# Attention's probabilities turned by DMA transposes of 16-bit halves instead of TensorE, two steps later, in a two-layer hybrid decoder trunk

## The chip, the cores and the metric

The kernel runs on one core of one Trainium2 chip. A core has TensorE (PE; its weight loads are listed apart as PEld), VectorE (DVE), ScalarE (ACT), GpSimd (POOL) and SyncE (SP, which here only issues DMAs); the on-chip memory SBUF with 128 partitions; and PSUM, where TensorE leaves its results. The metric is the device time of one execution in microseconds.

## The reference

Two layers over 512 tokens of width 1024, all float32. A layer is half a SwiGLU feed-forward (inner width 2816), then attention and a short convolution side by side behind one common projection, then another half feed-forward:

```python
x = x + 0.5 * swiglu(rms_norm(x, ffn1_norm[l]), ffn1_wg[l], ffn1_wu[l], ffn1_wd[l])
h = rms_norm(x, mix_norm[l])
z = h @ w_in[l]                      # q 8x64, k 2x64, v 2x64, conv B, C, h 512 each
attn_out = sliding_window_attention(q, k, v, attn_sink[l])
conv_out = short_conv(z[..., V_END:CB_END], z[..., CB_END:CC_END], z[..., CC_END:CH_END], conv_w[l])
x = x + jnp.concatenate([attn_out, conv_out], axis=-1) @ w_out[l]
x = x + 0.5 * swiglu(rms_norm(x, ffn2_norm[l]), ffn2_wg[l], ffn2_wu[l], ffn2_wd[l])
```

The attention has 8 query heads on 2 key heads and a window of 128 tokens, so a block of 128 queries sees its own block of keys and the one before it. A bias falls with distance, and each head has a learned sink in the denominator:

```python
scores = jnp.where(mask_b, scores + bias, -jnp.inf)
m = jnp.maximum(jnp.max(scores, axis=-1, keepdims=True), sink_l)
p = jnp.where(mask_b, jnp.exp(scores - m), 0.0)
denom = jnp.sum(p, axis=-1, keepdims=True) + jnp.exp(sink_l - m)
out = jnp.einsum("bnkgqs,bnskd->bnqkgd", p / denom, v_band)
```

## The kernel before

Activations lie with features on the partitions and tokens along the row. TensorE takes its operands as fp32r; each is split into a rounded part `hi` and a rest `lo`, and a product is made of three matmuls (hi·hi, lo·hi, hi·lo). `split` does this: ScalarE casts to `hi` (L223), VectorE subtracts to get `lo` (L224). For weights these tiles are called `wh` and `wl`, three buffers each.

Weights are loaded in 512 KB units into tiles `raw` of a pool of eight buffers (`stock`, tag "raw"). `need_raw` issues the loads on SP (L206) four units ahead of their split, and some on GpSimd's queue, which add to a tile that is there already (L218, L290). `take_split` asks for the split of a unit two groups before TensorE needs it.

The stage that the change touches is `mix`, once in each layer. `group` (L319, L320, L322) makes one 128-column block of the projection: 24 matmuls of 128x512 into one PSUM tile `acc`. The blocks come in the order k, v, four of q, and then twelve of the convolution (C, C, h, h, B, B for two pairs of blocks). After each block comes one "step" of attention, `attend(step)`; the steps from 6 on are made by `go_on`, which also asks for the next split, issued after the last instruction that `attend` returned.

Attention's work is cut into eight units (`Unit`, `todo`): key head g is 0 or 1 and query block n is 0 to 3, n running fastest. A unit has four heads. Its stages, each with a list of steps (`SCORES_AT`, `TURN_AT`, `VALUES_AT`), are:

- `scores`: 16 short matmuls into two PSUM tiles `sc`, VectorE adds the bias and takes the maximum (L1528), small VectorE instructions make `nm` and `es` (L1539, L1541), ScalarE takes the exponentials (L1545, and the sink's in L1548), VectorE adds up and inverts `sums` (L1549, L1550) and scales `p` (L1553). `p` is a tile of the "raw" pool, with queries on the partitions. It covers two blocks of keys, or one where n is 0.
- `turn`: keys have to lie on the partitions for the next product. For each block of keys, four TensorE transposes (L1561) bring `p` into PSUM `pt`, ScalarE casts it to `ph` (L1564), VectorE subtracts to `pl` (L1565).
- `values`: two matmuls for each block of keys (L1576, L1577) into `o`, ScalarE copies half of it to `ol` (L1579), VectorE adds both halves into `mixed` (L1582).

The convolution's elementwise work lies between: VectorE multiplies an `acc` into `cc` and `ch` (L1630, L1637), ScalarE and VectorE make the taps (L1639, L1641, L1642), GpSimd adds and scales (L1645, L1646), VectorE multiplies once more (L1650). Except in marked stretches, the order of each engine's instructions is laid down when the kernel is built, from priorities and assumed durations; at run time each engine takes its own in that order and waits on semaphores.

DMA transposes of 16-bit halves stand in the feed-forward already: `lay_apart` (L138, ScalarE) writes the two 16-bit halves of each word into two rows, a transpose is issued on SP for 1024 half words a partition (L1117), and ScalarE's copy (`join`, L1133) puts the halves together again.

Of the kernel before, what the change touches and what calls it, by code (L numbers as in the profile page):

```python
# [8 lines left out]
F32 = mybir.dt.float32  # L9
F32R = mybir.dt.float32r  # L10
BF16 = mybir.dt.bfloat16
U16 = mybir.dt.uint16
# [4 lines left out]
P = 128  # L17
# [36 lines left out]

SENT_AT = {3: (0, 0), 4: (1, 1)}
SCORES_AT = (5, 6, 7, 8, 9, 10, 12, 13)
TURN_AT = (6, 7, 8, 10, 11, 12, 14, 15)
VALUES_AT = (7, 8, 9, 11, 12, 13, 15, 16)
WARM = 3
XT_TAGS = ("sc", "aux", "aux", "mm", "sc", "sc", "aux", "aux")  # L60

# [11 lines left out]
def trunk_kernel(  # L73
# [23 lines left out]
    nc = tc.nc  # L97
# [8 lines left out]
    def psum(tag, shape, name):  # L106
        return ps.tile(shape, F32, tag=tag, bufs={"mm": 4, "sc": 2, "aux": 2}[tag], name=name)

    def g2(name, dt=F32, shape=(P, S)):
        return work.tile(list(shape), dt, tag="g2", bufs=14, name=name)  # L110

    def g8(name, dt=F32R, shape=(P, 2, 2, S)):
        return work.tile(list(shape), dt, tag="g8", bufs=4, name=name)
# [15 lines left out]
    def f32(ap):  # L129
        return ap.bitcast(F32)  # L130

    def words(ap):

        return ap.bitcast(U16).rearrange("p (n two) -> p two n", two=2)

    def lay_apart(src, name):
        halves = g2(f"halves_{name}", U16, (P, 2, S))
        nc.scalar.copy(halves, words(src))  # L138
        return halves
# [25 lines left out]
    ident = const.tile([P, P], F32, name="ident")  # L165
# [28 lines left out]
    state = {"raw": 0, "split": 0, "group": 0, "late": None}  # L194
# [673 lines left out]
    class Apart:  # L868
# [14 lines left out]
        def send(self, o, t):  # L883

            to = self.sent[o, t] = g8(f"turned_{self.name}_{o}_{t}", U16, (P, 2, NT, H))
            for u in range(2):
                halves = lay_apart(self.y[2 * t + u, o], f"{self.name}_{o}_{2 * t + u}")
                nc.sync.dma_start_transpose(
                    to.rearrange("p a c s -> p (a c) s")[:, :, u * P : (u + 1) * P],
                    halves.rearrange("p a n -> p (a n)"),  # L890
                )
# [572 lines left out]
    def mix(l, norm, after):  # L1464
        q = [None] * NH
# [39 lines left out]
        class Unit:  # L1505
# [7 lines left out]
            def scores(self):  # L1513
# [37 lines left out]
                for h in range(4):  # L1551
                    p = self.p[:, h, lo:]
                    nc.vector.tensor_scalar(p, p, sums[:, h : h + 1], None, op0=ALU.mult)  # L1553

            def turn(self):

                self.pt = []
                for kb in range(self.lo // P, 2):
                    tp = psum("aux", [P, 4, P], f"pt_{self.name}_{kb}")
                    for h in range(4):  # L1560
                        nc.tensor.transpose(tp[:, h, :], self.p[:, h, kb * P : (kb + 1) * P], ident)  # L1561
                    hi = g2(f"ph_{self.name}_{kb}", F32R, (P, 4, P))
                    lo = g2(f"pl_{self.name}_{kb}", F32R, (P, 4, P))
                    nc.scalar.copy(hi, tp)  # L1564
                    last = nc.vector.tensor_sub(lo, tp, f32(hi))  # L1565
                    self.pt.append((kb, hi, lo))
                return last

            def values(self):
# [11 lines left out]
                for r in range(2):  # L1581
                    nc.vector.tensor_add(  # L1582
                        f[r * HD : (r + 1) * HD], op[:HD, :, r, :], low[:, :, r, :]
                    )

        todo = [Unit(n, g) for g in range(NKV) for n in range(NT)]

        def attend(step):

            done = None  # L1590
            for at, stage in ((VALUES_AT, "values"), (TURN_AT, "turn"), (SCORES_AT, "scores")):
                if step in at:
                    done = getattr(todo[at.index(step)], stage)() or done
            return done

        for j in range(NH // 2):
            acc = group(norm.h) if j else qacc
            if j == 3:
                vv = take_values()
            qf = scaled(acc, f"qf_{l}_{j}", by=1.0 / 8.0)  # L1600
            both = form(f"q_{l}_{j}", shape=(P, 2, S))
            qe, qo = both[:, 0, :], both[:, 1, :]
            nc.scalar.copy(qe[:HD, :], qf[:HD, :])
            nc.scalar.copy(qo[HD:, :], qf[HD:, :])
            nc.vector.tensor_sub(qe[HD:, :], qf[:HD, :], f32(qe[:HD, :]))
            nc.vector.tensor_sub(qo[:HD, :], qf[HD:, :], f32(qo[HD:, :]))
            q[2 * j], q[2 * j + 1] = qe, qo
            attend(2 + j)
# [9 lines left out]
        def go_on():  # L1618

            nonlocal step  # L1620
            last = attend(step)
            step += 1
            with tc.issue_after(last.ins) if last else nullcontext():
                need_split(state["group"] - 1 + SPLIT_AHEAD)

        for pair in range(2):
            cs = []
            for j in range(2):
                c = g2(f"cc_{l}_{pair}_{j}")
# [4 lines left out]
            for j in range(2):  # L1634
                c = 2 * pair + j
# [39 lines left out]
    for l in range(DEPTH):  # L1675
        n1, n2, n3 = Norm(3 * l + 1), Norm(3 * l + 2), Norm(3 * l + 3)
        ffn(norm, INNER if l else FIRST, into(n1), None if l else make_bias)
        mix(l, n1, into(n2))
        if l + 1 < DEPTH:
            ffn(n2, INNER, into(n3))  # L1680
        else:
            ffn(n2, LAST)
        norm = n3
# [30 lines left out]
```

## Time and profile before

| | us |
|---|---|
| three runs | 1652.6, 1654.35, 1655.01; median 1654.35 |
| the profiled execution | 1655.83 |
| its span, from the first to the last instruction | 1654.1 |

| engine | busy, us | instructions |
|---|---|---|
| PE | 1636.2 | 8076 |
| DVE | 1381.4 | 1820 |
| ACT | 1107.9 | 1453 |
| POOL | 213.3 | 188 |

The profile is of one execution. Its page lists busy time by engine, the span in 40 slices, the DMA queues, the chain of work that ended last, and groups of instructions; the trace behind it answers by line, tile or window. A tile is named by what it is called in the program, `out<-in`. Matmuls are pipelined: one takes 0.39 us in the groups, but in a stream the next begins 0.23 us later, and the chain of work shows that pace. The mean granted clock of TensorE is 0.998. The first `mix` stage's attention lies at about 380 to 440 us of the span, the second's at about 1194 to 1274 us.

### The profile page before, as it was taken

The page shows a single profiled execution, that of the slowest core. Times are in us where ns is not written, and L with a number is a line of the kernel's source. Part 1 is how long each engine was busy: PE and PEld are TensorE (multiplying, and loading weights), DVE is VectorE, ACT ScalarE, POOL GpSimd, SP SyncE. Part 2 cuts the span into 40 slices and gives each one's busy share as a digit, 9 for nine tenths or more (in the row PEclk, how much of TensorE's full clock was granted, in tenths as well). Part 3 has the DMA queues.
Part 4 walks back from the last instruction along what each step waited for, and adds up shares of the span by engine and source line. Part 5 has one row for each costly group of instructions (what it writes and reads, how often), then busy time and mean ns, then how long its engine had stood idle before and what let it go on. Part 6 is the DMA issues. An engine that isn't in the chain of part 4 may idle for free.

```text
span 1654.1 us, 22072 instructions
## 1 busy us (share of the span) xinstructions
PE 1636.2 (99%) x8076; PEld 1382.2 (84%) x8076; DVE 1381.4 (84%) x1820; ACT 1107.9 (67%) x1453; POOL 213.3 (13%) x188
## 2 busy tenths in 40 slices
PE   9999999999999999999999999999999999999998
PEld 7888899988898888887888888878888988888876
DVE  7987779987899977797999777989788998777997
ACT  6447776565567577777665777786565766777655
POOL 0011111100221011111011111110012111111121
PEclk9999999999999999999999999999999999999999
DMA  8378997741397699989966989997125967999991
GB/s 256 88 193 213 226 220 194 185 122 52 96 229 181 180 216 214 215 203 221 230 150 171 226 211 219 226 221 205 52 65 132 228 150 186 224 223 224 236 248 73
DMA packets 277281, 306.10 MB, mean 185 GB/s; under 512 B 93805, under 2 KB 162485, under 8 KB 277173
## 3 DMA queue, kind: packets, MB, share of 16 engines
q1 hardware_dynamic: 236580, 222.24, 46.7%
q0 software_dynamic: 39872, 81.80, 28.8%
q8 instruction: 63, 1.03, 0.2%
q10 hardware_dynamic: 720, 0.66, 0.1%
q14 instruction: 46, 0.37, 0.1%
HBM read 262.71 MB, written 2.10 MB: 160 GB/s over the span
## 4 chain that ended last, share of the span: by engine, by line
PE 92%; DVE 4%; ACT 2%; issue 1%; DMA 1%; SPq 0%; DVEq 0%; ACTq 0%
PE x L825 25%; PE y L825 12%; PE acc L319 8%; PE acc L320 8%; PE acc L322 8%; PE w L825 6%; PE x_s L825 5%; PE x_m L810 3%; PE y_s L825 3%; PE x_s L810 2%; DVE wl L224 1%; PE y_s L810 1%; PE y_m L810 1%; PE x_e L825 1%; PE acc L705 1%
## 5 line engine op out<-in xcount | busy, mean ns | idle before, releaser
L223 ACT CAST wh<-raw 128x1024 fp32r<-128x1024 f32 (+1 forms) x491 | 512.1, 1045 | 387.5 <-PE x L825 94.0
L224 DVE TENSOR_TENSOR wl<-raw,wh 128x1024 fp32r<-128x1024 f32 (+1 forms) x491 | 596.4, 1221 | 169.0 <-ACT wh L223 168.3
L319 PE MATMUL acc<-xh,wh 128*128 128x512 f32 x424 | 165.8, 393 | 0.0
L320 PE MATMUL acc<-xl,wh 128*128 128x512 f32 x424 | 165.5, 390 | 0.0
L322 PE MATMUL acc<-xh,wl 128*128 128x512 f32 x416 | 162.2, 390 | 0.0
L218 POOL DMA_DIRECT2D raw<-in_ffn_wu_dram x39 | 48.7, 1249 | 401.2 <-DMA raw<-in_ffn_wu_dram 211.6
L320 PEld LDWEIGHTS acc<-xl,wh 128*128 128x128 f32 x424 | 79.7, 188 | 15.9 <-DVE xl L500 0.2
L319 PEld LDWEIGHTS acc<-xh,wh 128*128 128x128 f32 x424 | 79.8, 188 | 15.7
L322 PEld LDWEIGHTS acc<-xh,wl 128*128 128x128 f32 x416 | 78.1, 188 | 16.4
L1133 ACT COPY raw_a<-turned 128x1024 uint16<-128x1024 uint16 x64 | 83.8, 1357 | 0.0
L218 POOL DMA_DIRECT2D raw<-in_ffn_wg_dram x39 | 48.2, 1260 | 222.3 <-DMA raw<-in_ffn_wu_dram 82.8
L218 POOL DMA_DIRECT2D raw<-in_ffn_wd_dram x34 | 41.0, 1206 | 273.0 <-DMA raw<-in_ffn_wd_dram 185.5
L260 DVE TENSOR_TENSOR raw<-raw,raw 128x1024 f32<-128x1024 f32 x56 | 67.9, 1222 | 1.6 <-DMA raw<-in_ffn_wu_dram 1.0
L825 PE MATMUL w<-wh,fb21h 128*128 128x512 f32 x152 | 59.2, 390 | 0.0
L825 PE MATMUL x<-wh,ft2h 128*128 128x512 f32 x152 | 59.2, 390 | 0.0
L825 PE MATMUL y<-wh,ft3h 128*128 128x512 f32 x152 | 59.2, 390 | 0.0
L825 PE MATMUL x<-wl,ft1h 128*128 128x512 f32 x152 | 59.2, 389 | 0.0
L825 PE MATMUL w<-wl,fb21h 128*128 128x512 f32 x152 | 59.1, 389 | 0.0
L825 PE MATMUL x<-wl,ft2h 128*128 128x512 f32 x152 | 59.1, 389 | 0.0
L825 PE MATMUL x<-wh,ft1h 128*128 128x512 f32 x152 | 59.1, 389 | 0.0
L825 PE MATMUL w<-wh,fb21l 128*128 128x512 f32 x152 | 59.1, 389 | 0.0
L825 PE MATMUL x<-wh,ft2l 128*128 128x512 f32 x152 | 59.1, 389 | 0.0
(608 smaller groups left out, 4619.0 us busy)
## 6 DMA issues: line engine op xcount, KB each, us to landing
raw<-in_ffn_wu_dram SPq DMA_DIRECT2D x126, 512.0 KB, 5.2
raw<-in_ffn_wd_dram SPq DMA_DIRECT2D x105, 512.0 KB, 6.1
raw<-in_ffn_wg_dram SPq DMA_DIRECT2D x86, 512.0 KB, 5.4
raw<-in_ffn_wu_dram POOLq DMA_DIRECT2D x39, 512.0 KB, 8.2
raw<-in_ffn_wg_dram POOLq DMA_DIRECT2D x39, 512.0 KB, 6.3
raw<-in_w_in_dram SPq DMA_DIRECT2D x36, 512.0 KB, 3.7
raw<-in_ffn_wd_dram POOLq DMA_DIRECT2D x34, 512.0 KB, 8.9
raw<-raw POOLq DMA_DIRECT2D x21, 512.0 KB, 7.0
```

The source lines that it names most:

```text
L218: nc.gpsimd.dma_start(out=r, in_=rows_of(*more), accum_op=ALU.add)
L223: cast = nc.scalar.copy(hi, raw)
L224: eng.tensor_sub(lo, raw, f32(hi))
L260: nc.vector.tensor_add(a11, a11, s1)
L319: nc.tensor.matmul(acc, hi[:, k, :], rhs[k][0], start=k == first, stop=False)
L320: nc.tensor.matmul(acc, hi[:, k, :], rhs[k][1], start=False, stop=False)
L322: nc.tensor.matmul(acc, lo[:, k, :], rhs[k][0], start=False, stop=k == last)
L705: nc.tensor.matmul(opening[n], (lo if part == "w" else hi)[:, k, :], xl if part == "x" else xh, start=n not in begun, stop=k == KC - 1 and ...
L810: nc.tensor.matmul(accs[c // 2][:, c % 2, :], w[:, k, cols], x_[:, 2 * h + k, :], start=start and c % 2 == 0 and h + k + i == 0, stop=h + ...
L825: nc.tensor.matmul(accs[u], x_[:, 2 * h + k, tok], w[:, k, :], start=start and h + k + i == 0, stop=h + k == 2 and i == 2, skip_group_chec ...
L1133: nc.scalar.copy(words(raws[self.b][:, c, :]), self.to[:, :, c, :])
```

## The change

Six of the eight units, the first in `todo`, no longer go through TensorE to be turned. A new stage `send` stands one step behind `scores`: GpSimd copies the 16-bit halves of `p` apart into a half of a new tile `crossing` (units take turns between its two halves), and SP issues a DMA transpose from there back into the memory of `p`. In `turn`, now two steps behind `send`, ScalarE's `join` puts the halves of each block of keys together in `crossing`, issued after the latest weight cast; `ph` and `pl` are then made from there instead of from PSUM. `values` follows one step after `turn`. The last two units are still turned by TensorE, one after the other in steps 14 and 15, as before. `crossing` takes one buffer of the pool of four from which `mixed` comes.

```diff
+SEND_AT = (6, 7, 8, 9, 10, 11)
-TURN_AT = (6, 7, 8, 10, 11, 12, 14, 15)
-VALUES_AT = (7, 8, 9, 11, 12, 13, 15, 16)
+TURN_AT = (8, 9, 10, 11, 12, 13, 14, 15)
+VALUES_AT = (9, 10, 11, 12, 13, 14, 15, 16)
...
+            def send(self):
+                n = 4 * (2 * P - self.lo)
+                self.room = crossing[:, todo.index(self) % 2, :n]
+                halves = self.room.bitcast(U16).rearrange("p (two n) -> p two n", two=2)
+                nc.gpsimd.tensor_copy(
+                    halves.rearrange("p two (h k) -> p two h k", h=4),
+                    self.p[:, :, self.lo :].bitcast(U16).rearrange("p h (k two) -> p two h k", two=2),
+                )
+                self.turned = self.p.rearrange("p h k -> p (h k)").bitcast(U16)[:, : 2 * n]
+                nc.sync.dma_start_transpose(
+                    self.turned.rearrange("p (c q) -> p c q", q=P),
+                    halves.rearrange("p two n -> p (two n)"),
+                )
+
+            def join(self, kb):
+                at = kb - self.lo // P
+                whole = self.room[:, at * 4 * P : (at + 1) * 4 * P]
+                with tc.issue_after(state["cast"]):
+                    nc.scalar.copy(
+                        words(whole).rearrange("p two (h q) -> p two h q", h=4),
+                        self.turned.rearrange("p (two h k q) -> p k two h q", two=2, h=4, q=P)[:, at],
+                    )
+                return whole.rearrange("p (h q) -> p h q", h=4)
+
             def turn(self):
                 self.pt = []
                 for kb in range(self.lo // P, 2):
-                    tp = psum("aux", [P, 4, P], f"pt_{self.name}_{kb}")
-                    for h in range(4):
-                        nc.tensor.transpose(tp[:, h, :], self.p[:, h, kb * P : (kb + 1) * P], ident)
+                    if todo.index(self) < len(SEND_AT):
+                        tp = self.join(kb)
+                    else:
+                        tp = psum("aux", [P, 4, P], f"pt_{self.name}_{kb}")
+                        for h in range(4):
+                            nc.tensor.transpose(
+                                tp[:, h, :], self.p[:, h, kb * P : (kb + 1) * P], ident
+                            )
...
+        crossing = g8(f"crossing_{l}", F32, (P, 2, 4 * 2 * P))
...
-            for at, stage in ((VALUES_AT, "values"), (TURN_AT, "turn"), (SCORES_AT, "scores")):
+            for at, stage in (
+                (VALUES_AT, "values"), (TURN_AT, "turn"), (SEND_AT, "send"), (SCORES_AT, "scores")
+            ):
```

## The prediction

> **What bounds the kernel now.** I read the page's busy times and the chain of work that ended last, then the windows over the stage that changes, then the rows of its instructions.
>
> ```profile
> PE 1636.2 (99%) x8076; PEld 1382.2 (84%) x8076; DVE 1381.4 (84%) x1820; ACT 1107.9 (67%) x1453; POOL 213.3 (13%) x188
> PE 92%; DVE 4%; ACT 2%; issue 1%; DMA 1%; SPq 0%; DVEq 0%; ACTq 0%
> ```
>
> TensorE is the bound: the last chain runs through it for 92% of the span. The windows of the attention in the first layer (columns: length, then busy time of PE, PEld, DVE, ACT, POOL, clock, DMA share, GB/s), and two of the second:
>
> ```profile
> 380.00:400.00 20.00, 20.00 (x109) 17.11 (x108) 16.14 (x53) 12.10 (x29) 0.00 (x0) 1.00 0.11 32
> 400.00:420.00 20.00, 20.00 (x109) 17.01 (x108) 17.61 (x55) 14.83 (x40) 5.16 (x4) 1.00 0.21 59
> 420.00:440.00 20.00, 20.00 (x101) 16.78 (x99) 16.28 (x42) 9.02 (x25) 0.00 (x0) 1.00 0.28 83
> 1200.00:1220.00 20.00, 20.00 (x110) 16.95 (x110) 16.77 (x55) 12.53 (x33) 0.60 (x1) 1.00 0.18 54
> 1220.00:1240.00 20.00, 20.00 (x104) 16.91 (x103) 17.67 (x55) 11.65 (x36) 4.56 (x4) 1.00 0.25 75
> ```
>
> TensorE never rests here, so work taken from it is worth its full time as long as nothing new makes it wait. VectorE has 2.4 to 3.9 us in 20 left, ScalarE 5 to 11, GpSimd and the DMA engines nearly everything. The second layer looks the same, so I work out one layer and double it.
>
> **What is removed.** The pace of each kind of matmul is read from the chain in the order of time:
>
> ```profile
> 388.17 0.23 PE acc L320
> 394.13 0.23 PE o L1577
> 394.37 0.87 PE pt L1561 x8
> 395.36 0.12 PE sc L1525
> L1561 PE MATMUL pt<-ident,p x112: 270/272/327, 389.2 to 1267.8; 128*128 128x128 f32 x112
> ```
>
> Eight transposes hold TensorE 0.87 us, 0.109 each. Of the 112 transposes the six units had, in each layer, 10 blocks of keys with four heads: 40. That is 4.36 us a layer, 8.7 us in all, and the most that can be gained. By the same rows a group of 24 matmuls takes 5.52 us, a unit's 8 score matmuls 0.96, the `o` of a unit 0.92 (0.46 where it has one block of keys).
>
> **What is added, and its price.** For each sent unit: one GpSimd copy of 2048 half words (1024 for n = 0), one transpose on SP, one ScalarE join for each block of keys. The casts to `ph` and the subtractions to `pl` stay, from SBUF instead of PSUM.
>
> ```profile
> L1133 ACT COPY raw_a<-turned 128x1024 uint16<-128x1024 uint16 x64 | 83.8, 1357 | 0.0
> L1117 SPq DMA_TRANSPOSE turned<-halves x64: 1237/1243/4051, 123.4 to 1524.4; - x64
> DMA to landing us min/median/max: 2.7/5.0/8.6
> L168 POOL MEMSET ones<- 128x128 f32 x1 | 0.2, 205 | 0.0
> L1701 POOL MEMSET const-float32-1.0<- 128x1 f32 x1 | 0.1, 99 | 0.0
> L170 POOL CAST ones_r<-ones 128x128 fp32r<-128x128 f32 x1 | 0.3, 286 | 0.0
> L1646 POOL TENSOR_TENSOR cc<-cc,inv x8: 1283/1292/2172, 407.3 to 1271.4; 128x512 f32<-128x512 f32 x8
> ```
>
> A join is the same instruction as L1133: 1.36 us, ten a layer, 13.6 us on ScalarE. ScalarE has the time, but each stands in line before exponentials and weight casts.
>
> A transpose of 1024 half words landed 2.7 us after its issue at best and 5.0 at the median, where weights stream; here the DMA share is 0.1 to 0.3, so I take the best case, and for 2048 add an estimate of 1.1 us for the second 256 KB (the 1.5 us between the 1.24 of the issue and the 2.7, less some fixed latency): 3.8. The bounds are 2.7 and 8.6.
>
> No GpSimd copy of half words is in the trace. One fixed part of 0.10 us (the one-element memset) and the slope of the 128-element cast, (286-99)/128 = 1.46 ns an element, give 3.1 us for 2048 and 1.6 for 1024; I take these, since the cast is the nearest kind. The slope of the memset, 0.83 ns, gives 1.8 as lower bound; that of the two-input product, (1283-99)/512 = 2.3 ns, gives 4.8 as upper. The Trainium skill (GPSIMD Engine Reference, 4.1 Engine selection) has one-input operations at roughly line rate, an estimate of 1.7 us at its 1.2 GHz; by it the sum below would be some 8 us smaller.
>
> **The port.** When GpSimd works, VectorE's instructions with two inputs in SBUF stand still:
>
> ```profile
> L1541 DVE TENSOR_TENSOR es<-sink,nm x16: 152/161/668, 385.1 to 1258.1; 128x4 f32<-128x4 f32 x16
> L1549 DVE TENSOR_TENSOR sums<-sums,es x16: 152/164/1093, 387.7 to 1260.6; 128x4 f32<-128x4 f32 x16
> 415.47 1.29 POOL L1645 TENSOR_TENSOR cc<-cc,tap 128x511 f32<-128x511 f32 x1 [6.92 <-DVE tap L1642]
> 416.84 1.28 POOL L1646 TENSOR_TENSOR cc<-cc,inv 128x512 f32<-128x512 f32 x1
> 416.11 0.67 DVE L1541 TENSOR_TENSOR es<-sink,nm 128x4 f32<-128x4 f32 x1
> 417.05 1.09 DVE L1549 TENSOR_TENSOR sums<-sums,es 128x4 f32<-128x4 f32 x1 [0.27 <-ACT es L1548]
> ```
>
> `es` needs 0.16 us and took 0.67, ending at 416.78, just as GpSimd's instruction ended (416.76); `sums` then took 1.09 and ended at 418.14, with the second (418.12). So the one that comes later waits for the whole of the other. The Trainium skill says this of the shared port pair (SBUF — State Buffer, "Who interferes with whom"): an exclusive lock against a GpSimd instruction that reads SBUF; the trace agrees, and the rule speaks against this change. The copies are 4 x 3.1 + 2 x 1.6 = 15.6 us a layer, and VectorE's weight subtraction, `pl`, `es` and `sums` all fall under it.
>
> **Where it becomes late.** The stage gets a round trip in place of four transposes. The built order of the changed kernel has three places where ScalarE's queue puts the next unit's join ahead of what the previous one still lacks: the joins of unit 2 stand before the second `ph` of unit 1, those of unit 3 follow unit 2's `ph`, and unit 5's first join stands before the exponentials of unit 6. GpSimd's copy for a unit waits until the unit two before it is read out of its half of `crossing`; SP's transpose for unit 2 stands behind a weight load that waits for unit 1's join, because `p` holds one of the eight "raw" buffers longer. The other rows needed, from the groups of 365 to 430 us and the timeline:
>
> ```profile
> L224 DVE TENSOR_TENSOR wl<-raw,wh 128x1024 fp32r<-128x1024 f32 x9 | 11.0, 1222 | 0.2 <-ACT wh L223 0.2
> L223 ACT CAST wh<-raw 128x1024 fp32r<-128x1024 f32 x10 | 10.5, 1051 | 13.5 <-issue 13.5
> L1545 ACT ACTIVATE p<-p,nm 128x256 f32<-128x256 f32 x16 | 7.9, 498 | 8.6 <-DVE nm L1539 8.6
> L1548 ACT ACTIVATE es<-es 128x4 f32<-128x4 f32 x6 | 1.2, 192 | 0.5 <-DVE es L1541 0.5
> L1564 ACT CAST ph<-pt 128x512 fp32r<-128x512 f32 x8 | 4.4, 590 | 2.4 <-PE pt L1561 2.3
> L1565 DVE TENSOR_TENSOR pl<-pt,ph 128x512 fp32r<-128x512 f32 x8 | 5.2, 687 | 0.3 <-ACT ph L1564 0.2
> L1579 ACT COPY ol<-o 64x512 f32<-64x512 f32 x4 | 2.3, 586 | 0.1
> L1637 DVE TENSOR_TENSOR ch<-acc,cc 128x512 f32<-128x512 f32 x2 | 1.4, 692 | 1.2 <-PE acc L322 1.2
> 402.58 0.71 ACT L1639 ACTIVATE cc<-ch,par 128x512 f32<-128x512 f32 x1
> 403.19 0.71 ACT L1641 ACTIVATE tap<-ch,par 128x511 f32<-128x511 f32 x1
> ```
>
> First place, `o` of unit 1. From unit 0's `pl` on: two GpSimd products 2.58, copy for unit 2 3.1, its transpose 3.8, two joins 2.71, `ph` 0.59, `pl` 0.69: 13.5. TensorE from the same point does unit 0's `o` 0.46, scores 0.96, a group 5.52: 6.9. Unit 0's `pl` is early by the score matmuls and group before it (6.48) less `ch`, two taps, `ph`, `pl` (0.69+1.42+0.59+0.69 = 3.39): 3.1. TensorE waits 13.5-6.9-3.1 = 3.5. With the port, unit 1's copy (3.1) holds up unit 2's softmax and so `ch`, which uses up the 3.1 and makes unit 0's `o` 0.7 late, and a weight subtraction (1.22) gets between the two GpSimd products: 3.5+3.1+1.2+0.7 = 8.5.
>
> Second, `o` of units 2 and 3. From unit 1's last `pl`: copy 3.1, transpose 3.8, joins 2.71, `wh` 1.05, exponentials 4 x 0.50 + 0.19 = 2.2, `ol` 0.59, `ph` 0.59, unit 4's join 1.36, `ph` 0.59, `pl` 0.69: 16.7. TensorE: `o` 0.92, scores 0.96, group 5.52, `o` 0.92, group 5.52: 13.8. It waits 2.9, with the port (a weight subtraction ahead of the copy) 4.1.
>
> Third, `o` of unit 5. From unit 3's last `pl`: copy 3.1, transpose 3.8, join 1.36, exponentials 2.2, `ol` 0.59, `ph` 0.59, join 1.36, `wh` 1.05, `ph` 0.59, `pl` 0.69: 15.3. TensorE: 0.92+0.96+5.52+0.46+0.96+5.52 = 14.3. It waits 1.0, with the port 2.2.
>
> **The sum.** With the port 8.5+4.1+2.2 = 14.8 us of waits against 4.36 saved: +10.4 a layer, +20.9 in all. The two tap rows show that neighbours on an engine overlap (0.71 long, 0.61 apart); some five such links in each of six chains take off 3. That leaves +17.9: 1655.83 becomes 1673.7 in a profiled execution, or 1672 from the median of the three runs (1654.35), which is the time I give. The units' own delay, two steps further on, costs nothing beyond this, as `values` of the last two units keep steps 15 and 16.
>
> **Rivals.** (1) The round trip is late, but the port hardly matters (the copies fall into VectorE's idle stretches): waits 3.5+2.9+1.0 = 7.4, net +3.0 a layer, 1660. Against it: in the row above both of VectorE's small instructions that came under GpSimd were held, and the copies are two and a half times as long as that product. Chance 0.22.
>
> (2) All is hidden and TensorE keeps its gain: 1654.35-8.7 = 1645.6. This decides where copy plus transpose take less than half of the 6.9 us, for then the first chain fits under TensorE's work; DMA and GpSimd idle in the windows speak for it, but even the bests of both rows (1.8+2.7) leave a wait of 1.1 there without the port, and with it more. Chance 0.05. In between, with waits of 3 to 6 us a layer (the fast copy and no port: 7.4 less three times 1.3, 3.5), it comes out within 0.2%: 0.07.
>
> (3) The clock. TensorE stood still for parts of 260 to 266 us:
>
> ```profile
> 260.00:264.00 4.00, 2.43 (x19) 2.03 (x17) 4.00 (x5) 3.32 (x4) 1.53 (x2) 1.00 0.42 76
> 264.00:270.00 6.00, 5.18 (x30) 5.18 (x31) 5.54 (x6) 1.52 (x2) 0.26 (x1) 0.72 1.04 214
> ```
>
> After 2.4 us idle the granted clock fell to 0.72 of full over 6 us, that is 3.4 us at half: 1.7 us lost. Behind the 8.5 us wait that loss fits into the second wait; where it doesn't, or the later waits also drop the clock, two or three drops a layer add 7 to 10 us: 1680. [...] With the slow copy (4.8) as well, it passes 1690. Chance 0.06 for beyond 1690, the milder part lies in the forecast's range.
>
> **How the numbers follow.** The forecast's case has 0.60. The copy's bounds move three chains by -1.3 or +1.7 each: -8 or +10 in all; a landing at the 5.0 median adds 1.2 to each: +7. So that case runs from 1664 to 1690, and with rival (1) at 1660 the range is 1657 to 1690. Slower 0.60+0.22+0.06 = 0.88, same 0.07, faster 0.05; 0.2% is 3.3 us, about what runs of this kernel can tell from no change.
>
> **What would show it.** Right: 32 transposes left of 112; 12 GpSimd copies of 3.1 and 1.6 us; `es`, `sums`, `pl` or `wl` of VectorE stretched to 2 or 3 us under them; among the waits PE `o` on `pl`, 12 or more us in each layer, the longest at unit 1; ScalarE waiting for a DMA before a join; the clock under 1.00 in these windows. Wrong: TensorE without waits at `o`, or copies under 1.5 us.

## The result and the profile after

| | kernel before | kernel after |
|---|---|---|
| median of five runs, us | 1653.39 (1652.51 to 1655.01) | 1664.13 (1662.42 to 1666.1) |
| ratio, 95% interval | 1 | 1.0062 (1.0049 to 1.0075) |
| profiled execution: time, span, us | 1655.83, 1654.1 | 1662.79, 1660.8 |

The changed kernel is 10.7 us slower. The prediction said 1672, from 1657 to 1690: the direction and the range hold, the size is 8 us too large. The page after, its busy times and its last chain:

```profile
PE 1634.8 (98%) x7996; PEld 1373.8 (83%) x7996; DVE 1396.3 (84%) x1820; ACT 1130.3 (68%) x1473; POOL 238.5 (14%) x200
PE 84%; DVE 8%; ACT 4%; issue 2%; DMA 1%; POOL 1%; SPq 0%; ACTq 0%; DVEq 0%; POOLq 0%
```

TensorE has 80 instructions less, but its share of the last chain fell from 92% to 84%, and VectorE's rose from 4% to 8%: TensorE now waits for VectorE. Where, the windows of the attention show (length; busy time of PE, PEld, DVE, ACT, POOL; clock, DMA share, GB/s):

```profile
400.00:420.00 20.00, 17.05 (x73) 13.43 (x72) 19.61 (x47) 17.01 (x36) 11.39 (x6) 0.91 0.31 82
...
440.00:460.00 20.00, 18.25 (x88) 14.18 (x87) 16.48 (x37) 15.26 (x35) 5.92 (x4) 1.00 0.55 134
1220.00:1240.00 20.00, 17.29 (x74) 13.62 (x73) 19.59 (x48) 14.61 (x33) 11.78 (x7) 0.91 0.42 106
```

In 400 to 420 us TensorE rests for 3 us, VectorE is busy for 19.61 of 20 (17.61 before) with fewer instructions, GpSimd for 11.39 (5.16 before), and the clock is no longer full.

The whole attention is measured between two marks that both kernels have, the first score matmul of a layer and the first `x_m` matmul of the output product. In the timeline of before (start, length):

```profile
380.37 0.31 PE L1524 MATMUL sc<-kh,q 128*128 128x128 f32 x1
466.23 0.28 PE L810 MATMUL x_m<-fb11h_m,wh 128*128 128x256 f32 x1
```

and of after, both layers:

```profile
378.98 0.31 PE L1526 MATMUL sc<-kh,q 128*128 128x128 f32 x1
469.65 0.28 PE L812 MATMUL x_m<-fb11h_m,wh 128*128 128x256 f32 x1
1195.88 0.30 PE L1526 MATMUL sc<-kh,q 128*128 128x128 f32 x1
1286.85 0.28 PE L812 MATMUL x_m<-fb11h_m,wh 128*128 128x256 f32 x1
```

85.86 us became 90.67 in the first layer (+4.8), and 85.92 became 90.97 in the second (+5.05): 9.9 us. The 4.36 us of transposes a layer are gone, so 9.2 and 9.4 us of new waiting came in. The spans differ by only 6.7 us because this execution of before lost 1.7 us of clock at 265 us, which after did not (the last section says why), and TensorE's gaps at 757 to 777 us were 1.4 us shorter in after.

The instructions of the change, from the groups, the tile `crossing` and the DMA rows:

```profile
L1593 PE MATMUL pt<-ident,p x32: 270/272/273, 446.9 to 1272.9; 128*128 128x128 f32 x32
L1563 POOL COPY crossing<-p x12: 1031/1891/2820, 388.7 to 1249.1; 128x2048 uint16<-128x2048 uint16 x8, 128x1024 uint16<-128x1024 uint16 x4
L1578 ACT COPY crossing<-p x20: 1337/1356/1372, 393.0 to 1260.1; 128x1024 uint16<-128x1024 uint16 x20
DMA to landing us min/median/max: 2.7/3.7/3.8
L1599 DVE TENSOR_TENSOR pl<-crossing,ph 128x512 fp32r<-128x512 f32 x10 | 8.1, 817 | 0.5 <-ACT ph L1598 0.2
L1541 DVE TENSOR_SCALAR nm<-mx 128x4 f32<-128x4 f32 x8 | 4.0, 506 | 0.1
L1543 DVE TENSOR_TENSOR es<-sink,nm 128x4 f32<-128x4 f32 x8 | 2.9, 366 | 0.2
L1551 DVE TENSOR_TENSOR sums<-sums,es 128x4 f32<-128x4 f32 x8 | 3.0, 371 | 7.3 <-ACT es L1550 7.3
```

The copy of 2048 half words takes 1.89 us where nothing hinders it and up to 2.82 where it does. VectorE's small instructions of 0.16 us are at 0.37 to 0.51 on the mean of the first layer's eight. The longest wait, at `o` of unit 1, in the order of time:

```profile
404.43 2.25 POOL L1683 TENSOR_TENSOR cc<-cc,inv 128x512 f32<-128x512 f32 x1
405.47 1.25 DVE L1541 TENSOR_SCALAR nm<-mx 128x4 f32<-128x4 f32 x1
406.64 1.88 POOL L1563 COPY crossing<-p 128x2048 uint16<-128x2048 uint16 x1
406.75 1.79 DVE L1543 TENSOR_TENSOR es<-sink,nm 128x4 f32<-128x4 f32 x1
411.69 0.50 PE L1610 MATMUL o<-ph,vv 128*128 128x512 f32 x1
411.84 0.84 DVE L1616 TENSOR_TENSOR m<-o,ol 64x256 f32<-64x256 f32 x2
412.00 1.26 POOL L1682 TENSOR_TENSOR cc<-cc,tap 128x511 f32<-128x511 f32 x1 [3.48 <-DVE tap L1679]
412.34 2.55 ACT L1578 COPY crossing<-p 128x1024 uint16<-128x1024 uint16 x2 [0.70 <-DMA p<-crossing]
412.71 1.11 DVE L1599 TENSOR_TENSOR pl<-crossing,ph 128x512 fp32r<-128x512 f32 x1
413.87 0.51 PE L1611 MATMUL o<-pl,vv 128*128 128x512 f32 x1 [1.68 <-DVE pl L1599]
414.75 0.61 ACT L1598 CAST ph<-crossing 128x512 fp32r<-128x512 f32 x1
415.41 0.49 PE L1610 MATMUL o<-ph,vv 128*128 128x512 f32 x1 [1.03 <-ACT ph L1598]
416.13 0.52 PE L1611 MATMUL o<-pl,vv 128*128 128x512 f32 x1 [0.23 <-DVE pl L1599]
```

The engines take turns: `nm` ends as GpSimd's product ends (406.7) and `es` as the copy ends (408.5), so they lose 1.1 and 1.6 us. VectorE doesn't rest from there on, and comes to `pl` 1.0 us after `o`'s first matmul (411.69 to 412.71); there it loses another 0.4 us to the next GpSimd instruction (1.11 for 0.69). The second half of the wait is the one forecast: two joins for unit 2, themselves waiting for a transpose, stand ahead of unit 1's second `ph`. All waits of TensorE in the layer, 378 to 470 us (total, times, longest):

```profile
PE o L1611 <- DVE pl L1599: 2.4, 3, 1.7
PE acc L324 <- DVE wl L226: 1.3, 1, 1.3
PE o L1610 <- ACT ph L1598: 1.0, 1, 1.0
```

A wait counts some 0.16 us less here than it costs, since a matmul's row is 0.39 long at a pace of 0.23. With that and 1.7 us of lost clock the list makes 7.2 of the 9.2 us; the rest lies in gaps of 0.25 us and less. Two of the waits are not at unit 1: 0.5 of the 2.4 is at `o` of unit 6 (454 us), which TensorE still turns, and the 1.3 is behind it, for a weight subtraction that took 3.19 us where 1.22 is usual, under a product of the convolution. Both lie after 440 us, where the first-layer windows that the prediction read end; in before the last `o` of this layer is at 460 us.

### The profile page after: what moved, and what is told of

Read it like the earlier page. It is cut to its first block, busy times and chain, and to the rows that moved or that the text cites. A ratio compares the mean times of both kernels' runs of the same rounds, so it can differ in the third digit from the quotient of the medians.

```text
span 1660.8 us, 21973 instructions
## 1 busy us (share of the span) xinstructions
PE 1634.8 (98%) x7996; PEld 1373.8 (83%) x7996; DVE 1396.3 (84%) x1820; ACT 1130.3 (68%) x1473; POOL 238.5 (14%) x200
## 3 DMA queue, kind: packets, MB, share of 16 engines
q8 instruction: 63, 1.03, 0.2%
## 4 chain that ended last, share of the span: by engine, by line
PE 84%; DVE 8%; ACT 4%; issue 2%; DMA 1%; POOL 1%; SPq 0%; ACTq 0%; DVEq 0%; POOLq 0%
PE x L827 25%; PE y L827 12%; PE w L827 6%; PE acc L321 6%; PE acc L322 6%; PE acc L324 5%; PE x_s L827 5%; PE x_m L812 3%; PE y_s L827 3%; DVE wl L226 2%; PE x_s L812 2%; PE y_s L812 1%; PE y_m L812 1%; ACT p L1547 1%; PE x_e L827 1%
## 5 line engine op out<-in xcount | busy, mean ns | idle before, releaser
L827 PE MATMUL y<-wh,ft3l 128*128 128x512 f32 x152 | 59.1, 389 | 0.0
```

Of the source, the lines that this page charges most:

```text
L827: nc.tensor.matmul(accs[u], x_[:, 2 * h + k, tok], w[:, k, :], start=start and h + k + i == 0, stop=h + k == 2 and i == 2, skip_group_chec ...
```

## The experiments

Theory A is the forecast's chain: the round trip through DMA is too long, and ScalarE's order makes it worse. Theory B: what costs is the port that GpSimd's reads and VectorE's two-input instructions share, whoever waits for the copies. Theory C: the later steps themselves. Differences are to the kernel before in the same session; the attention is first score to first `x_m`, by layer.

| kernel | median us | to before | ratio, 95% interval | attention, us |
|---|---|---|---|---|
| before | | | | 85.86, 85.92 |
| later_only | 1655.48 | +0.4 | 1.0000 (0.9991 to 1.0009) | 86.81, 86.71 |
| copies_only | 1663.37 | +8.3 | 1.0049 (1.0037 to 1.0061) | 90.02, 90.55 |
| no_copy | 1654.76 | -0.4 | 0.9994 (0.9986 to 1.0003) | 84.87, 85.84 |
| unturned | 1653.61 | -1.5 | 0.9994 (0.9984 to 1.0003) | 84.75, 84.76 |
| unturned_quiet | 1650.77 | -4.4 | 0.9974 (0.9964 to 0.9985) | 82.48, 82.49 |
| copy_vector | 1660.82 | +5.7 | 1.0038 (1.0025 to 1.0051) | 88.19, 88.91 |
| copy_scalar | 1657.66 | +2.0 | 1.0016 (1.0006 to 1.0025) | 87.56, 88.13 |
| join_last | 1663.16 | +7.7 | 1.0049 (1.0036 to 1.0061) | 89.90, 90.38 |
| warm | 1673.75 | +18.6 | 1.0116 (1.0102 to 1.0130) | 95.66, 94.91 |
| alternate | 1659.14 | +4.0 | 1.0025 (1.0016 to 1.0035) | 86.17, 87.14 |
| three_vector | 1662.17 | +6.7 | 1.0036 (1.0023 to 1.0049) | 88.02, 90.30 |
| three_scalar | 1654.08 | -1.4 | 0.9998 (0.9988 to 1.0007) | 85.12, 85.10 |

**later_only.** TensorE turns all units; only the later steps stay.

```diff
-                    if todo.index(self) < len(SEND_AT):
+                    if False:
...
-                (VALUES_AT, "values"), (TURN_AT, "turn"), (SEND_AT, "send"), (SCORES_AT, "scores")
+                (VALUES_AT, "values"), (TURN_AT, "turn"), (SCORES_AT, "scores")
```

> TensorE turns all eight units as before; only the later steps of turn and values are kept. Theory A (the round trip is late, above all at unit 1, and its wait also brings a half-clock window): the later steps by themselves cost nothing, TensorE never waits, 1653.4 us as before, within 2. Theory B (GpSimd's copies hold VectorE at the shared port): the same, 1653.4. Theory C (the later steps by themselves hurt, through tiles that are held two steps longer): 1658 or more, with waits of TensorE in the windows of the attention.

No difference that can be told: theory C falls, though the attention is 0.9 and 0.8 us longer by the marks, through one wait of 0.8 us for a weight subtraction near its end.

**copies_only.** As later_only, with the copies made and read by nobody.

```diff
-                    if todo.index(self) < len(SEND_AT):
+                    if False:
...
-                self.turned = self.p.rearrange("p h k -> p (h k)").bitcast(U16)[:, : 2 * n]
-                nc.sync.dma_start_transpose(...)
```

> As the run with the later steps alone, and GpSimd also makes the six copies of each layer, which nobody reads: TensorE still turns the units. So the port is loaded as in the change, and no round trip is waited for. Theory A: VectorE's stretched instructions find room, at most 2 us more than the later steps alone, 1653 to 1656. Theory B: the stretched softmax makes TensorE wait, 5 us or more over the later steps alone, 1659 or more.

7.9 us more than later_only: theory B, and by more than its 5. In the timeline of copies_only the copies and GpSimd's products hold VectorE's two-input instructions one after the other:

```profile
403.11 1.89 POOL L1563 COPY crossing<-p 128x2048 uint16<-128x2048 uint16 x1 [4.46 <-DVE p L1555]
403.34 2.21 DVE L1674 SCALAR_TENSOR_TENSOR tap<-ch,par,tap 128x510 f32<-128x510 f32 x1
...
417.02 1.28 POOL L1678 TENSOR_TENSOR cc<-cc,inv 128x512 f32<-128x512 f32 x1
417.04 2.35 DVE L226 TENSOR_TENSOR wl<-raw,wh 128x1024 fp32r<-128x1024 f32 x1
```

The tap needs 0.75 us and took 2.21, the weight subtraction 1.22 and took 2.35, and TensorE waits for the second:

```profile
PE acc L324 <- DVE wl L226: 1.6, 3, 0.8
```

In this kernel `pl` reads PSUM, and its group shows it unhindered beside the same copies (0.688 us; 0.817 in after, where it reads `crossing`):

```profile
L1594 DVE TENSOR_TENSOR pl<-pt,ph 128x512 fp32r<-128x512 f32 x14 | 9.3, 688 | 0.4 <-ACT ph L1593 0.2
```

The Trainium skill (SBUF — State Buffer, "Who interferes with whom") has a VectorE instruction with two inputs in SBUF contend with a GpSimd instruction that reads SBUF; the two means agree.

**no_copy.** The changed kernel with `crossing` set to zero once in place of the copies.

```diff
-                nc.gpsimd.tensor_copy(halves ..., self.p ...)
...
+        nc.gpsimd.memset(crossing, 0.0)
         todo = [Unit(n, g) for g in range(NKV) for n in range(NT)]
```

> The changed kernel without GpSimd's copies: crossing is set to zero once in each layer, and transposes and joins go on as in the change (the probabilities of six units become zero). The chain is 1.9 us shorter and VectorE is free of the port. Theory A: a second ph of unit 1 still stands behind a join, so a wait of 1 to 2.5 us is left there in each layer in place of 3.9, and the clock drop goes or stays by the length of it: 1650 to 1657. Theory B: nothing is left to wait for, 1646 to 1650. Theory C: 1662 or more.

The copies are worth 11.1 us of the change (+10.7 against -0.4). The time lies in theory A's range and above theory B's 1646 to 1650, and without the copy the trip is also 1.9 us shorter, so this run alone doesn't decide between them; copies_only does, and copy_scalar below, which keeps the copy in the trip. TensorE waits 2.1 us in the first layer at `o` of unit 1, and that is not for transposes and joins, as the next two runs show.

**unturned.** No copy, no transpose, no join; `ph` and `pl` are made from `p`.

```diff
-                        tp = self.join(kb)
+                        tp = self.p[:, :, kb * P : (kb + 1) * P]
...
-                (VALUES_AT, "values"), (TURN_AT, "turn"), (SEND_AT, "send"), (SCORES_AT, "scores")
+                (VALUES_AT, "values"), (TURN_AT, "turn"), (SCORES_AT, "scores")
```

> The changed kernel without copies, transposes and joins: ph and pl of the six units are made from the probabilities as they lie, at the later steps (the turning of six units is left out). All theories but C: the 80 transposes are worth 8.7 us and nothing else waits, 1644.7 us, within 2. Theory C, or work of other engines that was hidden behind the transposes: over 1648.

7.2 us short of the 8.7, and within the interval of no change: since theory C has fallen, it is the last clause that holds, work of other engines that was hidden. The whole round trip of DMA and joins (no_copy less unturned) costs 1.1 us by the medians, no more than they can tell from nothing, but the 8.7 us of transposes do not come through without it either. The timeline of unturned has the same wait at unit 1:

```profile
412.74 1.28 POOL L1682 TENSOR_TENSOR cc<-cc,tap 128x511 f32<-128x511 f32 x1 [6.23 <-DVE tap L1679]
413.45 2.80 DVE L1599 TENSOR_TENSOR pl<-p,ph 128x512 fp32r<-128x512 f32 x2
414.10 1.60 POOL L1683 TENSOR_TENSOR cc<-cc,inv 128x512 f32<-128x512 f32 x1
414.62 0.50 PE L1611 MATMUL o<-pl,vv 128*128 128x512 f32 x1 [1.15 <-DVE pl L1599]
416.30 0.50 PE L1611 MATMUL o<-pl,vv 128*128 128x512 f32 x1 [0.95 <-DVE pl L1599]
```

Two `pl` took 2.80 us where two need 1.29: they now read SBUF twice and stand under the convolution's products on GpSimd, which were always there. With PSUM as source they were free of them (0.68 to 0.69 us, all 28 in copies_only).

**unturned_quiet.** As unturned, without these products.

```diff
-                nc.gpsimd.tensor_add(y[:, 1:], y[:, 1:], tap[:, 1:])
-                nc.gpsimd.tensor_mul(y, y, norm.inv)
```

> The run with six units not turned, and GpSimd's products of the convolution left out as well (the tap's addition and the norm's factor are missing). Theory B2 (pl, which reads two tiles in SBUF where it read PSUM before, now stands under GpSimd's products): the two waits of 1.2 and 1.0 us before o of unit 1 go in each layer, and the whole is 4 to 7 us under the unturned run: 1647 to 1650 on this chip. Rival D (the softmax work itself is late when TensorE comes sooner): the waits stay, 1652 or more.

2.8 us under unturned, 2.3 in each layer by the marks; the two `pl` take 1.29, and of the 2.1 us of waits 0.3 is left:

```profile
412.88 1.29 DVE L1599 TENSOR_TENSOR pl<-p,ph 128x512 fp32r<-128x512 f32 x2
413.63 0.50 PE L1611 MATMUL o<-pl,vv 128*128 128x512 f32 x1 [0.30 <-DVE pl L1599]
```

So the wait is the port's (B2), a little under the 4 to 7 us expected. The run also frees VectorE's other instructions of these products; the two `pl` themselves lost 1.5 us (2.80 against 1.29), and at most the 2.3 a layer can be put down to their move to SBUF. Even here only 3.4 of 4.36 us a layer come through.

**copy_vector** and **copy_scalar.** The changed kernel with the copy on another engine.

```diff
-                nc.gpsimd.tensor_copy(
+                nc.vector.tensor_copy(     (copy_scalar: nc.scalar.copy)
```

> The changed kernel with VectorE in GpSimd's place for the copy of half words: the same round trip, but nothing new at the shared port. Theory B (the port is what GpSimd's copies cost): near the run without copies, 1655 us, plus what the copy itself takes on VectorE (an estimate of 1 to 2 us each, five in each layer in full size, partly in its idle time): 1655 to 1661. Theory A (the length of the round trip): 1664 or more, as in the change, since the copy is no shorter than half of GpSimd's and VectorE has more to do.

> The changed kernel, all six units, with ScalarE in GpSimd's place for the copies (1.90 us for 2048 half words, as the run with three units on ScalarE showed). Nothing new reads through the shared port but pl. Theory B (port, of the copies and of pl): near the run without copies, 1655 us, plus what ScalarE's queue costs with some 10 us more in each layer: 1655 to 1659. Rival E (ScalarE, then busy for nine tenths of the attention, is late with exponentials and ph): 1661 or more.

Both land where theory B had them, copy_vector at the upper end. With ScalarE as the copier 8.7 of the 10.7 us go, though the copy is as long as on GpSimd and the transposes and joins remain; with VectorE 5.0 go. On ScalarE a copy takes as long as on GpSimd, on VectorE less, in the groups of the first layer of copy_scalar

```profile
L1563 ACT COPY crossing<-p 128x2048 uint16<-128x2048 uint16 x4 | 7.6, 1893 | 0.8 <-DVE pl L1599 0.8
```

and of copy_vector:

```profile
L1563 DVE COPY crossing<-p 128x2048 uint16<-128x2048 uint16 x4 | 5.6, 1393 | 0.0
```

Yet VectorE is the dearer copier, since VectorE is what TensorE waits for.

**join_last.** ScalarE's joins of a unit behind the second `ph` of the unit before.

```diff
-                with tc.issue_after(state["cast"]):
+                with tc.issue_after(state["cast"]), tc.issue_after(state.get("ph") or state["cast"]):
...
+                state["ph"] = done     # the last ph of this unit
```

> The changed kernel with ScalarE's joins of a unit queued behind the second ph of the unit before it, so the two joins of unit 2 no longer stand ahead of what o of unit 1 lacks; copies and port as in the change. Theory A (the order in ScalarE's queue is what makes the wait at unit 1): the second half of that wait (1.3+0.5 us in each layer) goes, and with it the half-clock window behind it: 4 to 7 us under the changed kernel, 1658 to 1661 us on this chip. Theory B (the port holds VectorE, and what waits is only a matter of who is next): the wait moves to unit 2 or to a weight subtraction: 1663 to 1667.

Theory B's number: 3.0 us under the changed kernel (+7.7 against +10.7). The wait for `ph` at unit 1 is gone, but `pl` is held there by the products (0.96 us in place of 1.03), and at 424 us a wait of 1.1 for a weight subtraction is new, beside the one of 1.4 behind `o` of unit 6. In its profile no half-clock window follows, and the attention is only 0.8 and 0.6 us shorter by the marks than in after, whose half speed alone cost 1.7 in each layer: the waits did not become less. TensorE's waits for weights in the first layer of join_last:

```profile
PE acc L324 <- DVE wl L226: 2.5, 2, 1.4
```

**warm.** 13 matmuls of zeros ahead of `o` of unit 1, to keep the clock up.

```diff
+                if todo.index(self) == 1:
+                    spin(13, op.rearrange("p a b q -> p (a b q)"))
```

> The changed kernel with 13 matmuls of zeros (0.227 us each, 2.95 us in all) ahead of o of unit 1 in each layer, written into the tile that o overwrites: they fill a wait of 3.9 us that the changed kernel has there. If the half-clock windows behind that wait come from the idleness: they go, 1.7 us gained for each, 3.4 us under the changed kernel, 1662 us on this chip. If they have another cause: no gain, 1664 to 1666, or more if the 13 matmuls don't fit into the wait.

It says nothing on the clock: the planner, which reckons with the matmuls, also put ScalarE's queue in another order, with a join of unit 3 ahead of unit 2's second `ph`. The timeline of warm shows what that costs:

```profile
427.56 1.33 ACT L1578 COPY crossing<-p 128x1024 uint16<-128x1024 uint16 x1 [4.72 <-DMA p<-crossing]
...
429.42 0.49 PE L1612 MATMUL o<-ph,vv 128*128 128x512 f32 x1 [2.95 <-ACT ph L1598]
```

So the mechanism of theory A exists; in after's own order it is only the second half of the wait at unit 1.

**alternate, three_vector, three_scalar.** Fewer units sent: 1, 3 and 5 with one step more (copies on GpSimd), or 2, 3 and 5, with the copies on VectorE or ScalarE and the others at the steps of before. The edits also name the units that are joined and their half of `crossing`.

```diff
-SEND_AT = (6, 7, 8, 9, 10, 11)
-TURN_AT = (8, 9, 10, 11, 12, 13, 14, 15)
-VALUES_AT = (9, 10, 11, 12, 13, 14, 15, 16)
+SEND_AT = (None, None, 8, 9, None, 11)      # alternate: (None, 7, None, 9, None, 11)
+TURN_AT = (6, 7, 10, 12, 11, 13, 14, 15)    # (6, 10, 8, 12, 11, 14, 13, 15)
+VALUES_AT = (7, 8, 11, 13, 12, 14, 15, 16)  # (7, 11, 9, 13, 12, 15, 14, 16)
```

> Only units 1, 3 and 5 go through the DMA, one step later still; units 0, 2 and 4 are turned by TensorE at the steps of the kernel before. 48 transposes go in place of 80: 5.2 us of TensorE's time. Theory A (the round trip is late): with one step more nothing waits, 1650 us. Theory B (port): half the copies, so half of their price (8 us for six units, so 4), and pl of three units under GpSimd's products: 1654 to 1658.

> Only units 2, 3 and 5 go through the DMA (their pl doesn't fall under GpSimd's products of the convolution), VectorE makes the copies, and the others are turned by TensorE at the steps of the kernel before. 48 transposes go: 5.2 us. Theory B (the price is the port): nothing of it is left but the copies on VectorE, which cost about 1 us for each unit when six were sent (6 us over the run without copies): 3 for three, 1653 us, 2 under the kernel before. Theory A: the trips of units 2 and 5 are late as in the forecast: 1657 or more.

> As the run with three units and VectorE's copies, but ScalarE makes the copies (an estimate of 2.7 us each from the join's 1.36 for half as many words), which leaves VectorE free and puts the copies in ScalarE's queue before exponentials. Theory B: ScalarE has 5 to 8 us left in 20 there, so nearly the whole 5.2 us comes through: 1650 to 1652. Rival E (ScalarE's queue holds up the exponentials): 1655 or more.

alternate lands 1 us above theory B's range, and tells less than meant: it turns unit 6 one step after its scores instead of two, and TensorE waits 1.5 us in each layer for that unit's `p`. three_vector is a miss by 9 us: from 400 to 420 us VectorE is full (columns as above),

```profile
400.00:420.00 20.00, 20.00 (x102) 16.93 (x101) 19.50 (x53) 15.41 (x39) 6.91 (x4) 1.00 0.42 106
```

while with the same schedule and ScalarE's copies it has 4 us left in three_scalar:

```profile
400.00:420.00 20.00, 20.00 (x101) 16.94 (x100) 15.55 (x56) 19.14 (x42) 5.17 (x4) 1.00 0.42 106
```

The two runs differ in the copier alone, and by 8.1 us (+6.7 against -1.4). That the full VectorE is the reason is argued: TensorE rests in neither window, and three_vector's waits come from 421 us on. three_scalar lies between the two times expected. It is the fastest version that leaves nothing out, 1.4 us under before by the medians and within what a measurement tells from no change (0.9988 to 1.0007). Of its 5.2 us, 1.6 come through by the marks; waits of 0.5 for a `pl` and 0.8 for a weight subtraction in each layer take part of the rest, and the remainder I can't place.

## Why the prediction came out as it did

**What was removed** is right in count (32 transposes left) and in TensorE's time, but "worth its full time as long as nothing new makes it wait" hid the point. With nothing put in the place of the transposes (unturned), 1.5 us of 8.7 come out. Up to 2.3 us a layer of what is missing go with GpSimd's products, since with them left out 3.4 of 4.36 come through by the marks. For the rest it is argued, not shown, that VectorE and TensorE were nearly level in this stage and the transposes were what VectorE caught up in. (A unit's scores are 8 matmuls, as the sum has it: the traces have 64 in each layer. The 16 given ahead of the prediction is wrong.)

**The prices.** Join 1.36 us and landing 2.7 and 3.7 us are as forecast (3.8). The GpSimd copy is the mis-sized term: 1.89 and 1.03 us where 3.1 and 1.6 were taken. It follows the slope of the memset, (1891-1031)/1024 = 0.84 ns a half word, my lower bound (1.8), not that of the cast. The Trainium skill's line rate (GPSIMD Engine Reference, 4.1 Engine selection) had given an estimate of 1.7 and a sum 8 us smaller; the measured 1.89 is nearer to that than to 3.1. With 1.9 in three chains, 1.2 us off each, my own sum would be 7 us lower: 1665. That it then meets 1664 is in part chance, for the waits do not lie where the sum had them:

- **First place, `o` of unit 1:** forecast 8.5. Measured 2.18 us from `o`'s first matmul to its second (411.69 to 413.87), 1.54 to the third and 0.72 to the fourth, at a pace of 0.23 each: 3.8 us of waiting. The round trip makes only the later 1.8 of it. Of the first 1.95, 1.0 is VectorE coming late to `pl`, after `nm` and `es` of unit 3 had lost 2.7 us under a product and unit 2's copy, and 0.4 is `pl` under the tap's addition; join_last has the same 1.95, and unturned, with no copy, 1.3. A softmax held up by a copy was in the sum, one unit earlier.
- **Second place, units 2 and 3:** forecast 4.1, no wait in the trace of after. Third, unit 5: forecast 2.2, measured 0.2.
- **Not foreseen:** 0.6 us at `o` of unit 6, which TensorE still turns, 1.4 at the weight subtraction behind it, and the clock counting in full. The sign of 12 us or more of waits in each layer is not met: all new waiting, the clock with it, is 9.2.

**The port** is right as the main cause, but both shares of the sum are too large. The sum gave the port 7.4 us a layer (14.8 against 7.4); the copies alone, with no one waiting for them, cost 7.9 in both layers together. The round trip by itself was given the other 7.4 a layer; in both layers together the DMA trip and joins cost 1.1 (no_copy less unturned), and 3.5 with a copy on ScalarE ahead of them (copy_scalar less unturned). Two things were missed. The lock reaches further than `es`, `sums`, `pl` and `wl`: `nm`, which has one input, and the tap are held too. And the sentence that the subtractions to `pl` "stay, from SBUF instead of PSUM" passed over what that costs by itself: up to 2.3 us a layer (unturned against unturned_quiet), under GpSimd work that the kernel had before.

**The clock.** I let the loss fit into the second wait. There was no second wait, so it counted in full: half speed from 416.49 to 419.90 and from 1232.27 to 1235.69 us in the profiled execution, 1.7 us lost each time. TensorE need not be idle through a whole window for it: 2.06 us of 3.42 were enough at 413.07 (last section).

**Rivals.** Rival (1), the port hardly matters, 1660, has a time nearer than the forecast's (4 us under where that is 8 over), and is refuted all the same by copies_only. Rival (2), all hidden, falls with unturned: even with no round trip at all nothing near 1645.6 comes out. Rival (3) is part of the cause, in its mild form.

In all, from run to run: the transposes taken out with the source of `pl` moved to SBUF -1.9 us (unturned less later_only), the DMA trip and joins +1.1 (no_copy less unturned), the copies on GpSimd +11.1, of which 8.7 is GpSimd's being the copier and 2.4 any copy at all, on ScalarE (copy_scalar less no_copy). The last sum mixes sessions; each number is against the kernel before of its own, and the 1.9 and the 1.1 are about what the medians can tell from nothing.

## What to carry to other kernels

Before work is taken from the bound engine, look at how far the next engine is behind it: here VectorE was busy for 17.6 of 20 us, and 8.7 us taken from TensorE were worth 1.5 with nothing put in their place, and 4.4 with GpSimd's products left out as well. Where an operand moves from PSUM to SBUF, or GpSimd gets a reading job, list every VectorE instruction with two inputs in SBUF beside it; ScalarE made the same copy in the same time for 8.7 us less. A DMA transpose that lands after 3.7 us was cheap here when issued two steps ahead of its use; what stands ahead of its consumer in a queue that a planner orders can still make it dear, as warm shows.

## What the runs showed of the hardware

**The clock looks at fixed windows.** All changes of clock in a trace lie on a grid of 3.413 us. Three windows on that grid in after: 1.35 us idle at 263 us, and the two at unit 1 of the first layer:

```profile
262.89:266.30 3.41, 2.06 (x15) 1.86 (x16) 3.41 (x4) 1.98 (x2) 1.46 (x2) 1.00 0.74 144
413.07:416.49 3.42, 1.35 (x4) 0.68 (x5) 3.14 (x7) 3.42 (x10) 2.15 (x3) 1.00 0.10 28
416.49:419.90 3.41, 3.41 (x14) 3.02 (x13) 3.41 (x5) 3.41 (x9) 2.47 (x1) 0.50 0.42 126
```

and the one of before that lost its clock at 265 us:

```profile
261.93:265.34 3.41, 1.26 (x8) 1.06 (x9) 3.41 (x4) 2.74 (x3) 1.79 (x2) 1.00 0.51 100
```

In the 14 traces of this study, leaving out their first and last 10 us, every window in which TensorE was idle for 1.92 us or more (15 of them) was followed by one at half speed, none with 1.59 or less was (but for one that followed a half-speed window), and of ten between 1.63 and 1.85 six were. Where the grid falls differs from run to run: before and after have the same two idle stretches of 1.0 and 1.35 us at 262 to 265, in one window in before (2.15 idle, half speed follows) and in two in after (no drop). That is 1.7 us of scatter for each such place, and the runs of after show it: 1662.4 and 1662.8 us at a mean clock of 0.997, 1664.1 to 1666.1 at 0.994 and 0.995.

**The lock works both ways and passes from one to the other.** GpSimd's product needs 1.28 us and took 2.25 beside VectorE's weight subtraction; the copy took 2.82 for 1.89. An instruction of 0.16 us (`es`) took 1.79.

**Copies of 16-bit halves.** 2048 of them, read at a stride of two: 1.89 us on GpSimd, 1.89 on ScalarE, 1.39 on VectorE, by the rows above.
